# An expert's rows: gather products on TensorE, or an indirect DMA and transposes

## The chip, the cores and the metric

The kernel runs on one core of one Trainium2 chip. The metric is device microseconds from start to end of one execution; the median of three runs of the kernel before is 1578.53 us (1578.49 to 1578.84). The engines are TensorE (PE, with its weight loads as PEld), VectorE (DVE), ScalarE (ACT), GpSimd (POOL) and SyncE (SP). Each works through a queue of its own in order, and semaphores tie the queues together.

## The reference

A streaming encoder block on 512 tokens of width 1024. Attention, a recurrence and a first LayerNorm make `h`, 512 x 1024. Then comes the part that the change touches, a mixture of 32 experts of which each token uses four:

```python
logits = xt @ w_router + b_router
top_logit, top_e = lax.top_k(logits, 4); gate = softmax(top_logit)
# for each expert e, over the rows (tokens) that chose it:
hb = xb @ w_up[e] + b_up[e]                     # 1024 -> 2048
glu, lin = split(hb); glu = min(glu, 7); lin = clip(lin, -7, 7)
act = glu * sigmoid(1.702 * glu) * (lin + 1)
y = act @ w_down[e] + b_down[e]                 # 1024 -> 1024
out[token] += gate * y
h = layer_norm(ALPHA * h + out, ln2_g, ln2_b)
```

All of it is in float32; the weights of the 32 experts are 384 MB.

## The kernel before

**Slots.** Each expert has 128 slots, 32 for each of four blocks of 128 tokens. `posm` holds, for a token and an expert, the slot; `onehot` compares it with the slot numbers and makes `oh` for a group of four experts (`GRP`). `meta` multiplies `oh` with a small table `vals` and so gets each slot's token number (`idx`) and gate; an empty slot has a number above 511, which the indirect DMA skips.

**Rows.** `gather(k, n)` multiplies `h1` (128 of its 1024 columns) with `oh` for four experts at once, which gives the rows of these experts already transposed in PSUM. ScalarE writes the high part `xh[k]` and VectorE the remainder `xl[k]`, both in a 32-bit format that TensorE takes in one pass; three products (high x high, high x low, low x high) stand for one in float32 (`mm3`). For the first group the gather steps lie between the first expert's chunks; for a later group they lie in the last expert of the group before (`more`).

**Weights.** `Stream` brings the weights in chunks of 1 MB (128 x 2048) by SP into raw tiles: four of pool a, `RAW_B` = 2 and `RAW_C` = 1. An expert has eight up chunks and four down chunks; the order is up of expert e, then down of e - 1. A chunk is split by a ScalarE cast (line 88, high) and a VectorE subtract (line 90, low) into one of four pairs of tiles. `ahead(c)` puts the splits up to chunk c + 2 into the queues, and `raw` tiles set free take the next loads.

**The order in an expert.** `up_begin` starts four PSUM sums of 512 columns with a bias product each (line 401); `up_chunk` adds 12 products for each of eight chunks (lines 396 to 398). After chunk k come, in this order, `ahead(up[k])` and one step of `act_gen` of the expert before: transposes of its activation (`act_T`, lines 435, 438, 439) in two halves. Then `dn_half` adds the four down chunks of the expert before, twelve products each; behind chunk k come `ahead` and then a step of `act_gen` for the present expert: `act0` reads two sums on ScalarE (lines 419, 420), `act1` finishes on VectorE (lines 426 to 428), for half 0 and half 1. `u_buf`, one tile, is shared by both halves, so line 419 of half 1 waits for line 428 of half 0. `finish` scales the result on ScalarE (line 456) and POOL adds it into `acc` in DRAM by an indirect DMA (line 457). `final_tiles` prepares the last LayerNorm in raw tiles that are free once all weights are loaded.

**Before the experts.** A written order (`B_ORDER`) weaves the first LayerNorm, the router and the first four weight splits. `start_acc` scales a block of `h` on ScalarE into a tile `sl` and POOL stores it as the start of `acc`.

The instructions of all this are issued in program order on each engine, as written.

Of the kernel before, what the change touches and what calls it, by code (L numbers as in the profile page):

```python
# [157 lines left out]
class Moe:  # L158
    def __init__(self, tc, ctx, a, cst, ne=NE):
        self.tc, self.nc, self.a, self.c, self.ne = tc, tc.nc, a, cst, ne  # L160
        nc = tc.nc
        self.dram = ctx.enter_context(tc.tile_pool(name="moe_dram", bufs=1, space=DRAM))
        self.acc = self.dram.tile([T, D], F32, name="acc_dram")
        self.tab_f = self.dram.tile([128, 2], F32, name="tab_f")
        self.tab_i = self.dram.tile([128, 2], I32, name="tab_i")
        self.bias = ctx.enter_context(tc.tile_pool(name="moe_bias", bufs=1)).tile([128, 2048], BF, name="bias")

    def open_routing(self, ctx):
        tc = self.tc
        keep = ctx.enter_context(tc.tile_pool(name="moe_keep", bufs=1))  # L170
        self.small = ctx.enter_context(tc.tile_pool(name="moe_small", bufs=2))
        self.lg = keep.tile([128, NB, NE], F32, name="lg")
        self.mx = keep.tile([128, NB, 8], F32, name="mx")
        self.sel = keep.tile([128, NB, NE], BF, name="sel")
        self.posm = keep.tile([128, NB, NE], F32, name="posm")
        self.vals = keep.tile([128, NB, NE, 5], BF, name="vals")
        self.hT = {}
        self.n_i = keep.tile([128, 1], I32, name="n_i")
        hp = ctx.enter_context(tc.tile_pool(name="moe_h", bufs=1))
        self.hp = hp  # L180
        self.sl = [self.slot(b, [128, D], F32) for b in range(NB)]

    def slot(self, b, shape, dt):

        return self.hp.tile(shape, dt, name=f"sl{b}")
# [151 lines left out]
    def open(self, ctx, h1):  # L337
        tc, nc = self.tc, self.nc
        self.h1 = h1
# [6 lines left out]
        self.xh = [self.xp.tile([128, 128 * GRP], F32R, name=f"xh{k}", bufs=1) for k in range(8)]  # L346
        self.xl = [self.xp.tile([128, 128 * GRP], F32R, name=f"xl{k}", bufs=1) for k in range(8)]
# [3 lines left out]
        self.ohT = self.xh[0].rearrange("p (b t) -> p b t", b=NB)  # L351
# [7 lines left out]
    def meta(self, n, vals_of):  # L359

        nc = self.nc
        pm = self.ps_tr.tile([128, 4, 128], F32, name="ps_tr", tag="tr")
        ohb = self.oh.bitcast(BF).rearrange("p b e (j two) -> p b e j two", two=2)
        for i in range(n):
            for b in range(NB):
                nc.tensor.matmul(pm[SLB * b:SLB * b + SLB, 0, 8 * i:8 * i + 5], ohb[:, b, i, :, 1], vals_of(b, i),
                                 start=True, stop=True)
        yield
        m = self.xp.tile([128, GRP, 5], F32, name="meta")
        nc.vector.tensor_copy(m[:, 0:n], pm[:, 0, 0:8 * n].rearrange("p (i s) -> p i s", i=n)[:, :, 0:5])  # L370
        t = self.xp.tile([128, GRP], F32, name="meta_t")
        idx = self.xp.tile([128, GRP], I32, name="idx")
        nc.vector.scalar_tensor_tensor(t[:, 0:n], m[:, 0:n, 1], -BIG, m[:, 0:n, 0], op0=ALU.mult, op1=ALU.add)
        nc.vector.tensor_scalar(idx[:, 0:n], t[:, 0:n], self.c.base, None, op0=ALU.add)
        gate = self.xp.tile([128, GRP], F32, name="gate_s")
        nc.vector.tensor_reduce(gate[:, 0:n], m[:, 0:n, 2:5], axis=AX.X, op=ALU.add)
        self.where += [(idx[:, i:i + 1], gate[:, i:i + 1]) for i in range(n)]
# [31 lines left out]
    def up_chunk(self, ps, i, w, k):  # L409
        wh, wl = w  # L410
        xh, xl = (x[k][:, 128 * i:128 * i + 128] for x in (self.xh, self.xl))
# [97 lines left out]
    def slots_T(self, idx):  # L509

        nc = self.nc
        row = self.xp.tile([128, NB], F32, name="row")
        for b in range(NB):
# [46 lines left out]
    def experts(self, out):  # L560
# [7 lines left out]
        self.where = []  # L568
# [3 lines left out]
        def slots(e):  # L572
            self.onehot(self.posm[:, :, e:e + GRP], GRP)

        def rows(e):
            yield from self.meta(GRP, lambda b, i: self.vals[:, b, e + i, :])

        def act_gen(ps):
# [8 lines left out]
            t = [self.act_T(h) for h in range(2)]  # L587
            next(t[0])
            yield
            next(t[0])  # L590
            next(t[1])
            yield
            next(t[1])
            yield
# [6 lines left out]
        act = meta = iter(())  # L601
        for e in range(ne + 1):
            first, i = e == 0, e % GRP
            if e < ne:
                up = self.up_c[e]
                more = i == GRP - 1 and e + 1 < ne
                ps_up = self.up_begin(self.sel_of(e))
                gs = deque()
                for k in range(8):
                    if first and k < 7:  # L610
                        g = self.gather(k + 1, GRP)
                        next(g)
                    self.up_chunk(ps_up, i, st.get(up[k]), k)
                    if first and k < 7:
                        next(g)
                    ahead(up[k])
                    next(act, None)
                    if gs:
                        next(gs.popleft())
                    if more:  # L620
                        gs.append(self.gather(k, GRP))
                        next(gs[0])
                    if first and k == 0:
                        self.gate_parts()
                    if first and k in (1, 2, 3, 4):
                        self.start_acc(k - 1)
                    if first and k == 6:
                        meta = rows(0)
                    if i == GRP - 2 and k == 0 and e + 2 < ne:
                        slots(e + 2)  # L630
                        meta = rows(e + 2)
                    if k > 5:
                        next(meta, None)
            else:
                drain(act)
            if first:
                act = act_gen(ps_up)
                self.ah, self.al = (self.slot(b, [128, 8, 128], F32R) for b in (0, 1))
                self.y = self.slot(2, [128, D], F32)
                self.overflow_list(self.ps_tr, "tr")  # L640
                for _ in range(3):
                    next(act)
                continue
            ps = self.dn_begin()
            nxt = act_gen(ps_up) if e < ne else iter(())
            for k in range(4):
                w = st.get(self.dn_c[e - 1][k])
                self.dn_half(ps, w, k, 0)
                self.dn_half(ps, w, k, 1)
                ahead(self.dn_c[e - 1][k])  # L650
                if k < 3:
                    next(nxt, None)
                if k == 0 and gs:
                    next(gs.popleft())
            act = nxt
            if e < ne:
                self.finish(ps, *self.where[e - 1])
                self.added = e == ne - 1
        for _ in final:
            pass  # L660
        idx, gate = self.where[-1]
# [3 lines left out]
    def overflow(self, out):  # L665
# [3 lines left out]
        with tc.For_i(0, n, 1) as i:  # L669
# [23 lines left out]
            idx, gate = self.where[-1]  # L693
            for k in range(8):
                drain(self.gather(k, 1))
# [14 lines left out]
            for k in range(8):  # L710
                self.up_chunk(ps, 0, chunk(self.up_src(wu, k)), k)
# [891 lines left out]
RAW_B = 2  # L1603
RAW_C = 1
# [10 lines left out]
def build(tc, a, out):  # L1615
    nc = tc.nc
    with ExitStack() as ctx:
# [14 lines left out]
        with ExitStack() as c2:  # L1632
# [10 lines left out]
            def block(b):  # L1643
# [4 lines left out]
                def norm():  # L1648
                    ln.mean()
                    yield  # L1650
                    ln.squares(xb, moe.sl[b])
# [12 lines left out]
                def rest():  # L1664
# [6 lines left out]
                    ln.rest(xb, 1)  # L1671
                    yield
# [20 lines left out]
        with ExitStack() as c2:  # L1693
            st.grow([pool(c2, f"w_raw_c{i}", 1, "right", reuse_waits="tile") for i in range(RAW_C)])
            c2.enter_context(tc.manual_schedule())
            moe.open(c2, x)
# [17 lines left out]
```

## Time and profile before

| what | value |
| --- | --- |
| median of three runs | 1578.53 us |
| the profiled execution, its own time | 1581.11 us |
| its span, first to last instruction | 1579.3 us, mean granted clock 0.984 |
| TensorE busy | 1506.9 us (95%) |
| VectorE busy | 1321.6 us (84%) |
| ScalarE busy | 1077.5 us (68%) |
| HBM read | 430.48 MB, 287 GB/s over the span |
| plain POOL DMA issue (line 506) | 0.55 us of POOL |

The page gives busy time, share of the span and the number of instructions for each engine. TensorE's matmuls overlap each other, so its busy share says whether there are holes, not how near it is to its peak. Times in the trace count from the first instruction. The expert stage begins at 336.5 us (the first bias products) and the last down product of expert 30 starts at 1530.05 us.

### The profile page before, as it was taken

What the parts mean: (1) busy time and instruction counts of PE and PEld (TensorE: products, weight loads), DVE (VectorE), ACT (ScalarE), POOL (GpSimd) and SP (SyncE); (2) the same over time, 40 slices, a digit from 0 to 9 for tenths busy, and PEclk for the clock granted to TensorE, in tenths of its full rate; (3) what the DMA queues carried; (4) which work ended last, traced back from release to release, by engine and by line L of the source; (5) the groups of instructions that cost most, each with busy time, mean ns of one, the idle gap of its engine ahead of it and who ended that gap; (6) DMA issues with size and microseconds to landing.
All of it is one profiled execution on the core that took longest, in us unless ns stands there. A gap on an engine that the chain in (4) does not pass through costs nothing. (4 is left out here: it accounts for less than half of the span.)

```text
span 1579.3 us, 20360 instructions
## 1 busy us (share of the span) xinstructions
PE 1506.9 (95%) x7609; PEld 1243.3 (79%) x7641; DVE 1321.6 (84%) x1519; ACT 1077.5 (68%) x1148; POOL 163.2 (10%) x213
## 2 busy tenths in 40 slices
PE   7999999998999999999999999999999999999994
PEld 5888998876778878778878788878877887877873
DVE  8867877678888888889889979988988888888885
ACT  4678452456767777777677777777776777777762
POOL 5120413210000000000000000000000000000023
PEclk9999999999999999999999999999999999999997
DMA  5222117338898998899899979997999899889973
GB/s 194 90 71 67 28 41 271 138 138 298 336 338 309 368 372 308 335 364 356 299 353 352 359 280 366 369 368 282 374 371 332 311 371 373 311 336 363 353 257 113
DMA packets 95546, 446.67 MB, mean 283 GB/s; under 512 B 11407, under 2 KB 22072, under 8 KB 62674
## 3 DMA queue, kind: packets, MB, share of 16 engines
q1 hardware_dynamic: 86002, 425.51, 70.5%
q0 software_dynamic: 7488, 19.00, 4.9%
q8 instruction: 62, 1.02, 0.3%
q10 hardware_dynamic: 1952, 0.80, 0.2%
q14 instruction: 42, 0.34, 0.1%
HBM read 430.48 MB, written 22.55 MB: 287 GB/s over the span
## 5 line engine op out<-in xcount | busy, mean ns | idle before, releaser
L90 DVE TENSOR_TENSOR w_lo_t<-w_raw,w_hi_t 128x2048 fp32r<-128x2048 f32 (+1 forms) x392 | 877.9, 2269 | 155.5 <-ACT w_hi_t L88 155.5
L88 ACT CAST w_hi_t<-w_raw 128x2048 fp32r<-128x2048 f32 (+1 forms) x392 | 736.0, 1897 | 102.9 <-PE ps_up_t L398 88.7
L396 PE MATMUL ps_up_t<-w_hi_t,xh 128*128 128x512 f32 x1024 | 419.5, 410 | 0.0
L398 PE MATMUL ps_up_t<-w_hi_t,xl 128*128 128x512 f32 x1024 | 402.1, 393 | 0.0
L397 PE MATMUL ps_up_t<-w_lo_t,xh 128*128 128x512 f32 x1024 | 400.6, 391 | 0.0
L396 PEld LDWEIGHTS ps_up_t<-w_hi_t,xh 128*128 128x128 f32 x1024 | 193.2, 189 | 53.2 <-ACT sl L456 17.3
L398 PEld LDWEIGHTS ps_up_t<-w_hi_t,xl 128*128 128x128 f32 x1024 | 192.7, 188 | 44.4
L397 PEld LDWEIGHTS ps_up_t<-w_lo_t,xh 128*128 128x128 f32 x1024 | 193.3, 189 | 37.5
L396 PE MATMUL ps_dn_t<-w_hi_t,sl 128*128 128x512 f32 x512 | 202.7, 396 | 0.5 <-ACT sl L438 0.5
L398 PE MATMUL ps_dn_t<-w_hi_t,sl 128*128 128x512 f32 x512 | 201.4, 393 | 0.0
L397 PE MATMUL ps_dn_t<-w_lo_t,sl 128*128 128x512 f32 x512 | 200.8, 392 | 0.0
L457 POOL DMA_INDIRECT acc_dram<-sl,idx x31 | 48.5, 1563 | 1095.9 <-ACT sl L456 1041.6
L419 ACT ACTIVATE act_u<-ps_up_t 128x512 f32<-128x512 f32 x64 | 38.0, 594 | 130.0 <-DVE act_l L428 130.0
L398 PEld LDWEIGHTS ps_dn_t<-w_hi_t,sl 128*128 128x128 f32 x512 | 96.7, 189 | 22.0 <-DVE sl L439 0.3
L396 PEld LDWEIGHTS ps_dn_t<-w_hi_t,sl 128*128 128x128 f32 x512 | 96.9, 189 | 21.1 <-ACT sl L438 0.9
L397 PEld LDWEIGHTS ps_dn_t<-w_lo_t,sl 128*128 128x128 f32 x512 | 96.8, 189 | 21.0
L390 ACT CAST xh<-ps_tr 128x512 fp32r<-128x512 f32 x64 | 37.6, 588 | 66.1 <-PE ps_tr L386 66.1
L386 PEld LDWEIGHTS ps_tr<-oh,h 128*128 128x128 f32 x512 | 66.0, 191 | 6.0 <-DVE xl L391 1.3
L386 PE MATMUL ps_tr<-oh,h 128*128 128x128 f32 x512 | 68.4, 276 | 0.1
L438 ACT CAST sl<-ps_tr 128x512 fp32r<-128x512 f32 x64 | 37.5, 587 | 36.5 <-PE ps_tr L435 35.8
L919 PE MATMUL pj<-mw_hi,hT 128*128 128x256 f32 (+1 forms) x192 | 60.5, 315 | 1.6 <-ACT hT L1040 1.3
L920 PE MATMUL pj<-mw_lo,hT 128*128 128x256 f32 (+1 forms) x192 | 58.6, 306 | 1.1 <-DVE mw_lo L847 1.1
(360 smaller groups left out, 1786.4 us busy)
## 6 DMA issues: line engine op xcount, KB each, us to landing
w_raw<-in_w_up SPq DMA_DIRECT2D x256, 1024.0 KB
w_raw<-in_w_down SPq DMA_DIRECT2D x128, 1024.0 KB
mw_raw<-in_w_in SPq DMA_DIRECT2D x16, 512.0 KB
w_raw<-in_w_o SPq DMA_DIRECT2D x4, 1024.0 KB
mw_raw<-in_w_in SPq DMA_DIRECT2D x4, 672.0 KB
h_dram<-x POOLq DMA_DIRECT2D x4, 512.0 KB, 3.5
h<-h_dram POOLq DMA_DIRECT2D x4, 512.0 KB, 10.8
acc_dram<-sl POOLq DMA_DIRECT2D x4, 512.0 KB, 3.5
```

What stands on the lines that cost most here:

```text
L88: self.nc.scalar.copy(h[:, s], r[:, s])
L90: self.nc.vector.tensor_sub(l[:, s], r[:, s], h[:, s].bitcast(F32))
L386: nc.tensor.matmul(p[:, 0:n, SLB * b:SLB * b + SLB], self.h1[b][:, 128 * k:128 * k + 128], self.oh[:, b, 0:n, :], start=True, stop=True)
L390: nc.scalar.copy(self.xh[k][:, 0:128 * n], pf)
L396: mm(ps, xh, wh, start=start, stop=False)
L397: mm(ps, xh, wl, start=False, stop=False)
L398: mm(ps, xl, wh, start=False, stop=stop)
L419: nc.scalar.activation(self.u_buf, ps[h], AF.Sigmoid, scale=SW_ALPHA)
L438: nc.scalar.copy(ah[:, s, :], p)
L457: nc.gpsimd.indirect_dma_start(out=self.acc[:, :], out_offset=bass.IndirectOffsetOnAxis(ap=idx[:, :1], axis=0), in_=y, in_offset=None, bou ...
L919: mm(ps, xh, wh, start=start, stop=False, skip_group_check=True)
L920: mm(ps, xh, wl, start=False, stop=False, skip_group_check=True)
```

## The change

- Each block of `h` is stored to DRAM (`store_rows`, a DMA on POOL at the end of its LayerNorm). An expert's rows are fetched from there by `fetch`, an indirect DMA on POOL into one of two tiles `xg`, cleared at first; an empty slot leaves what stood there. The fetch of expert e + 1 is issued at the start of expert e; those of 0 and 1 before the first.
- `x_T` transposes the fetched rows in two blocks of four on TensorE; ScalarE and VectorE write `xh` and `xl` of that expert. It runs in the up chunks of the expert before (`turn`: first the two halves of `act_T`, then those of `x_T`, then `meta` of the next group).
- `gather` is gone. `meta` can give the index alone or the gate alone.
- After a chunk, up or down, the step (`turn`, or `halves` with `act0` and `act1`) now comes ahead of `ahead(...)`, that is, ahead of that chunk's weight split in the queues.
- The tiles `sl` are gone: `start_acc` scales `h1` in place, and the activation's tiles take the place of `h1`. `RAW_B` is 4 and `RAW_C` 2, so there are ten raw tiles in place of seven.

```diff
+    def store_rows(self, b, h):
+        self.nc.gpsimd.dma_start(self.rows[128 * b:128 * b + 128, :], h)
...
     def start_acc(self, b):
-        x = self.slot(b, [128, D], F32)
-        self.nc.scalar.mul(x, self.h1[b], ALPHA)
+        x = self.h1[b]
+        self.nc.scalar.mul(x, x, ALPHA)
         self.nc.gpsimd.dma_start(self.acc[128 * b:128 * b + 128, :], x)
...
+        self.xg = [self.xp.tile([128, D], F32, name=f"xg{i}", bufs=1) for i in range(2)]
+        for x in self.xg:
+            nc.gpsimd.memset(x, 0.0)
...
-    def gather(self, k, n):
-        p = self.ps_tr.tile([128, 4, 128], F32, name="ps_tr", tag="tr")
-        for b in range(NB):
-            nc.tensor.matmul(p[:, 0:n, SLB * b:SLB * b + SLB], self.h1[b][:, 128 * k:128 * k + 128],
-                             self.oh[:, b, 0:n, :], start=True, stop=True)
-        yield
-        pf = p.rearrange("p e t -> p (e t)")[:, 0:128 * n]
-        nc.scalar.copy(self.xh[k][:, 0:128 * n], pf)
-        nc.vector.tensor_sub(self.xl[k][:, 0:128 * n], pf, self.xh[k][:, 0:128 * n].bitcast(F32))
-        yield
+    def fetch(self, e, idx):
+        self.nc.gpsimd.indirect_dma_start(
+            out=self.xg[e % 2], out_offset=None, in_=self.rows[:, :],
+            in_offset=bass.IndirectOffsetOnAxis(ap=idx[:, :1], axis=0), bounds_check=T - 1, oob_is_err=False)
+
+    def x_T(self, e):
+        xh, xl = (self.xp.tile([128, 8, 128], F32R, name=nm) for nm in ("xh", "xl"))
+        self.x[e] = xh, xl
+        for q in range(2):
+            p = self.ps_tr.tile([128, 4, 128], F32, name="ps_tr", tag="tr")
+            for i in range(4):
+                k = 4 * q + i
+                nc.tensor.transpose(p[:, i, :], self.xg[e % 2][:, 128 * k:128 * k + 128], self.c.ident)
+            yield
+            s = slice(4 * q, 4 * q + 4)
+            nc.scalar.copy(xh[:, s, :], p)
+            nc.vector.tensor_sub(xl[:, s, :], p, xh[:, s, :].bitcast(F32))
+            yield
...
+        def turn():
+            if e:
+                t = [self.act_T(h) for h in range(2)]
+                next(t[0])
+                yield
+                next(t[0])
+                next(t[1])
+                yield
+                next(t[1])
+                yield
+            if e + 1 < ne:
+                t = self.x_T(e + 1)
+                next(t)
+                yield
+                next(t)
+                next(t)
+                yield
+                next(t)
+                yield
+            if first:
+                yield from meta(0, idx=False)
+            if e % GRP == 1 and e + GRP < ne:
+                slots(e // GRP + 1)
+                yield from meta(e // GRP + 1)
 
         slots(0)
+        drain(meta(0, gate=False))
+        for e in range(2):
+            self.fetch(e, self.idx[e])
         st.split_to(self.up_c[0][0] + FIRST_SPLIT)
-        g = self.gather(0, GRP)
-        next(g)
-        next(g)
+        drain(self.x_T(0))
         for e in range(ne + 1):
...
+                if e and e + 1 < ne:
+                    self.fetch(e + 1, self.idx[e + 1])
                 ps_up = self.up_begin(self.sel_of(e))
                 for k in range(8):
-                    self.up_chunk(ps_up, i, st.get(up[k]), k)
+                    self.up_chunk(ps_up, self.x[e], st.get(up[k]), k)
...
+                    next(steps, None)
                     ahead(up[k])
-                    next(act, None)
...
             for k in range(4):
                 w = st.get(self.dn_c[e - 1][k])
                 self.dn_half(ps, w, k, 0)
                 self.dn_half(ps, w, k, 1)
+                next(act, None)
                 ahead(self.dn_c[e - 1][k])
-                if k < 3:
-                    next(nxt, None)
...
-RAW_B = 2
-RAW_C = 1
+RAW_B = 4
+RAW_C = 2
...
                     ln.rest(xb, 1)
+                    moe.store_rows(b, xb)
                     yield
```

## Rows read from the trace of the kernel before

**Rows 1.** The page's busy time, share and instructions of each engine.

```profile
PE 1506.9 (95%) x7609; PEld 1243.3 (79%) x7641; DVE 1321.6 (84%) x1519; ACT 1077.5 (68%) x1148; POOL 163.2 (10%) x213
```

**Rows 2.** Table by stage, four experts: stretch, length, busy per engine, granted clock, DMA, GB/s.

```profile
1010.02:1045.52 35.50, 35.25 (x171) 28.25 (x172) 32.21 (x26) 26.82 (x21) 1.55 (x1) 1.00 0.96 363
1045.52:1089.38 43.86, 42.59 (x219) 35.28 (x220) 35.94 (x29) 30.30 (x29) 1.54 (x1) 1.00 0.83 298
1089.38:1124.93 35.55, 34.84 (x155) 28.14 (x156) 31.60 (x21) 27.03 (x22) 1.55 (x1) 1.00 0.93 359
1124.93:1160.07 35.14, 34.88 (x155) 28.15 (x156) 31.19 (x21) 26.58 (x21) 1.54 (x1) 1.00 0.96 368
```

**Rows 3.** Timeline of TensorE around a transpose block: start, length, instruction.

```profile
1013.53 0.40 PE L398 MATMUL ps_up_t<-w_hi_t,xl 128*128 128x512 f32 x1
...
1014.44 0.39 PE L397 MATMUL ps_up_t<-w_lo_t,xh 128*128 128x512 f32 x1
```

**Rows 4.** Timeline of TensorE: down products and next bias products; idle and releaser in brackets.

```profile
1034.30 0.39 PE L396 MATMUL ps_dn_t<-w_hi_t,sl 128*128 128x512 f32 x1
...
1042.77 0.39 PE L397 MATMUL ps_dn_t<-w_lo_t,sl 128*128 128x512 f32 x1
...
1045.06 0.40 PE L398 MATMUL ps_dn_t<-w_hi_t,sl 128*128 128x512 f32 x1
1045.52 0.59 PE L401 MATMUL ps_up_t<-bias,erow_b 128*128 128x512 bf16 x2
1046.29 0.38 PE L401 MATMUL ps_up_t<-bias,erow_b 128*128 128x512 bf16 x1 [0.17 <-DVE act_u L426]
```

**Rows 5.** Timeline of ScalarE around the end of the same expert.

```profile
1031.35 1.92 ACT L88 CAST w_hi_t<-w_raw 128x2048 fp32r<-128x2048 f32 x1 [0.83 <-PE ps_up_t L398]
...
1033.81 0.60 ACT L420 ACTIVATE act_l<-ps_up_t 128x512 f32<-128x512 f32 x1
1034.50 1.92 ACT L88 CAST w_hi_t<-w_raw 128x2048 fp32r<-128x2048 f32 x1
1040.44 0.60 ACT L419 ACTIVATE act_u<-ps_up_t 128x512 f32<-128x512 f32 x1 [4.02 <-DVE act_l L428]
...
1041.41 3.71 ACT L88 CAST w_hi_t<-w_raw 128x2048 fp32r<-128x2048 f32 x2
1045.01 1.27 ACT L456 ACTIVATE sl<-ps_dn_t,gate_s 128x512 f32<-128x512 f32 x2
```

**Rows 6.** Timeline of VectorE in the same stretch.

```profile
1036.45 2.29 DVE L90 TENSOR_TENSOR w_lo_t<-w_raw,w_hi_t 128x2048 fp32r<-128x2048 f32 x1 [0.20 <-ACT w_hi_t L88]
1038.66 0.68 DVE L426 SCALAR_TENSOR_TENSOR act_u<-ps_up_t,act_u 128x512 f32<-128x512 f32 x1
...
1043.35 2.29 DVE L90 TENSOR_TENSOR w_lo_t<-w_raw,w_hi_t 128x2048 fp32r<-128x2048 f32 x1 [2.94 <-ACT w_hi_t L88]
```

**Rows 7.** From issue to landing: the accumulates of line 457, the loads of line 506.

```profile
DMA to landing us min/median/max: 6.0/7.2/7.6
...
DMA to landing us min/median/max: 4.2/5.6/7.0
```

**Rows 8.** Timeline of VectorE and TensorE at the start of the expert stage.

```profile
334.38 0.69 DVE L356 TENSOR_TENSOR oh<-posm,slots 128x512 f32<-128x512 f32 x1
335.54 1.13 PE L386 MATMUL ps_tr<-oh,h 128*128 128x128 f32 x8
...
338.17 0.48 PE L396 MATMUL ps_up_t<-w_hi_t,xh 128*128 128x512 f32 x1
```

**Rows 9.** Table by stage, columns as in rows 2, around two falls of the clock.

```profile
35.30:39.50 4.20, 1.43 (x9) 1.10 (x9) 3.83 (x7) 1.78 (x8) 2.54 (x2) 1.00 0.00 0
39.60:42.90 3.30, 3.30 (x14) 3.25 (x13) 2.36 (x13) 1.74 (x5) 1.54 (x2) 0.50 0.01 2
367.40:370.60 3.20, 0.03 (x1) 0.00 (x0) 2.75 (x18) 0.00 (x0) 0.00 (x0) 1.00 0.99 355
370.70:377.40 6.70, 4.44 (x11) 2.91 (x11) 5.44 (x8) 4.67 (x4) 0.00 (x0) 0.50 0.35 132
```

**Rows 10.** Timeline of TensorE before the last transposes.

```profile
1533.47 0.64 PE L497 MATMUL ps_tr<-ident,w_raw 128*96 128x128 f32 x4 [3.02 <-POOL w_raw L485]
```

More of the change, by code (lines that the diff above doesn't have):

```diff
@@ L178, in open_routing @@
         self.n_i = keep.tile([128, 1], I32, name="n_i")
[L179 to L181 removed]
     def slot(self, b, shape, dt):
[L185 removed]
+        return self.h1_pool.tile(shape, dt, name=f"h1_{b}")
+    def store_rows(self, b, h):
+        self.nc.gpsimd.dma_start(self.rows[128 * b:128 * b + 128, :], h)
     def load_consts(self, pool):
@@ L371, in meta @@
[L371 to L377, printed above, removed]
@@ new lines, in meta @@
+        if idx:
+            t = self.xp.tile([128, GRP], F32, name="meta_t")
+            x = self.xp.tile([128, GRP], I32, name="idx")
+            nc.vector.scalar_tensor_tensor(t[:, 0:n], m[:, 0:n, 1], -BIG, m[:, 0:n, 0], op0=ALU.mult, op1=ALU.add)
+            nc.vector.tensor_scalar(x[:, 0:n], t[:, 0:n], self.c.base, None, op0=ALU.add)
+            self.idx += [x[:, i:i + 1] for i in range(n)]
+        if gate:
+            g = self.xp.tile([128, GRP], F32, name="gate_s")
+            nc.vector.tensor_reduce(g[:, 0:n], m[:, 0:n, 2:5], axis=AX.X, op=ALU.add)
+            self.gate += [g[:, i:i + 1] for i in range(n)]
@@ L567, in ahead, with meta, slots, halves @@
                 next(final, None)
-        self.where = []
+        self.idx, self.gate = [], []
         self.added = False
         ne = self.ne
[L572 to L578, printed above, removed]
+        def meta(g, **parts):
+            yield from self.meta(GRP, lambda b, i: self.vals[:, b, GRP * g + i, :], **parts)
+        def slots(g):
+            self.onehot(self.posm[:, :, GRP * g:GRP * g + GRP], GRP)
+        def halves(ps):
             self.act0(ps, 0)
@@ L596, in experts @@
         slots(0)
+        drain(meta(0, gate=False))
+        for e in range(2):
+            self.fetch(e, self.idx[e])
         st.split_to(self.up_c[0][0] + FIRST_SPLIT)
-        g = self.gather(0, GRP)
-        next(g)
-        next(g)
-        act = meta = iter(())
+        drain(self.x_T(0))
         for e in range(ne + 1):
-            first, i = e == 0, e % GRP
+            first = e == 0
+            steps = turn()
             if e < ne:
                 up = self.up_c[e]
-                more = i == GRP - 1 and e + 1 < ne
+                if e and e + 1 < ne:
+                    self.fetch(e + 1, self.idx[e + 1])
@@ L623, in experts @@
+                    if first and k in (1, 2, 3, 4):
+                        self.start_acc(k - 1)
+                    if first and k == 5:
+                        self.ah, self.al = (self.slot(b, [128, 8, 128], F32R) for b in (0, 1))
+                        self.y = self.slot(2, [128, D], F32)
+                    next(steps, None)
+                    ahead(up[k])
                     if first and k == 0:
                         self.gate_parts()
-                    if first and k in (1, 2, 3, 4):
-                        self.start_acc(k - 1)
@@ L627, in experts @@
[L627 to L635, printed above, removed]
+                del self.x[e]
+            drain(steps)
             if first:
-                act = act_gen(ps_up)
-                self.ah, self.al = (self.slot(b, [128, 8, 128], F32R) for b in (0, 1))
-                self.y = self.slot(2, [128, D], F32)
@@ L640, in experts @@
                 self.overflow_list(self.ps_tr, "tr")
-                for _ in range(3):
-                    next(act)
+                drain(halves(ps_up))
                 continue
             ps = self.dn_begin()
-            nxt = act_gen(ps_up) if e < ne else iter(())
+            act = halves(ps_up) if e < ne else iter(())
             for k in range(4):
@@ L649, in experts @@
                 self.dn_half(ps, w, k, 1)
+                next(act, None)
                 ahead(self.dn_c[e - 1][k])
-                if k < 3:
-                    next(nxt, None)
-                if k == 0 and gs:
-                    next(gs.popleft())
-            act = nxt
             if e < ne:
-                self.finish(ps, *self.where[e - 1])
+                self.finish(ps, self.idx[e - 1], self.gate[e - 1])
                 self.added = e == ne - 1
@@ L660, in experts @@
             pass
-        idx, gate = self.where[-1]
+        idx, gate = self.idx[-1], self.gate[-1]
         self.slots_T(idx)
@@ L692, in overflow @@
             drain(self.meta(1, lambda b, _: vals[:, b, :]))
-            idx, gate = self.where[-1]
-            for k in range(8):
-                drain(self.gather(k, 1))
+            idx, gate = self.idx[-1], self.gate[-1]
+            self.fetch(0, idx)
+            drain(self.x_T(0))
             et = self.xp.tile([128, NE], F32, name="ov_et")
```

48 lines of the change are left out of this document (15 added, 33 removed).

## The prediction

> **What bounds the kernel now.** I read the page first: TensorE is busy 95% of the span [rows 1]. Its matmuls overlap, so that share proves nothing yet. The table by stage comes next: from 409.93 to 1495.40 us the kernel repeats one pattern of four experts, 35.50, 43.86, 35.55 and 35.14 us long, 150.05 together [rows 2]. The long one makes the gather products for the next four. The timeline of TensorE says what fills a plain expert: from 1034.30 to 1045.06 there are 47 steps of 0.229 us without a hole [rows 4]. An expert has 96 up and 48 down products, 144 x 0.229 = 33.0 of 35.14 us; bias products, eight transposes and a short wait are the rest. So in this stage TensorE's own queue sets the time. VectorE's 31 to 32 us and ScalarE's 27 us lie beneath, and so do the weight loads: 368 GB/s in the plain expert, and yet no hole.
>
> How near the other engines are is the question; the view for it is the timeline of ScalarE and of VectorE around an expert's end [rows 5, 6]. The down products begin at 1034.30. ScalarE's cast at 1031.35 is that of down chunk 2; line 420 waits until 1033.81 for the last up sums that it reads; the cast at 1034.50 is chunk 3's; then line 419 waits 4.02 us for VectorE, which first subtracts chunk 3 (1036.45) and then runs lines 426 to 428 (from 1038.66). VectorE in turn waits 2.94 us for the next cast. TensorE sees none of it, because chunks 2 and 3 were sent ahead of these waits.
>
> **What is removed: the gather.** In the steady stage seven experts make 64 products each. Such an expert costs 43.86 - 35.14 = 8.72 us more than a plain one [rows 2], with the switches and a wait at the transposes in it. 7 x 8.72 = **-61.0 us**; the first expert's 56 products are in the start, below. ScalarE and VectorE gain nothing: eight 128x512 evacuations for four experts become two for each.
>
> **What is added: transposes.** `x_T` makes two blocks of four transposes an expert, in the shape of `act_T`. From the product at 1013.53 through such a block to the second product behind it, at 1014.44, is 0.91 us, where two plain steps take 0.46 [rows 3]. So 2 x 0.455 = 0.91 us in each of experts 1 to 30: **+27.3 us**. The index and gate products only move.
>
> **The fetch.** An indirect DMA per expert stands on POOL's queue right behind the accumulate of line 457. That one lands 7.2 us after its issue, at most 7.6 [rows 7]; it issues after the sums of 1045.01 [rows 5], about when up chunk 0 starts. The fetch, 1.55 us later on the queue [rows 2], is read after up chunk 3, some 12 us into the up products. Even if it lands 4.4 us behind the accumulate it fits, so I cost it at nothing; without that cover each us late is 30 us. More raw tiles only deepen a prefetch that is ahead already: nothing.
>
> **The moved evacuations: a gain.** `up_begin` waits for the last sums now: the third bias product starts at 1046.29, 0.77 us after the first, where two steps take about 0.44 [rows 4], so 0.33 is lost; after a gather expert it is another 0.41 (35.55 against 35.14). Sums that no longer stand behind one VectorE subtract (2.2 us) cover both. 30 x 0.33 + 7 x 0.41: **-13 us**.
>
> **The moved evacuations: a new wait.** In the new order ScalarE's queue at an expert's end is: sums of half 0, cast chunk 2, sums of half 1, cast chunk 3. VectorE's is: subtract 2, lines 426 to 428, subtract 3. Each piece waits for the one before it, and the first waits for TensorE's up sums. Forward from 1033.81 with the durations of [rows 5, 6]:
> - line 420 until its successor can start, 0.48 (half of 1040.44 to 1041.41): chunk 2's cast starts at 1034.29, not at 1031.35;
> - cast 1.92, subtract 2.21: line 426 at 1038.43;
> - lines 426 to 428 and the hand-over, 1.78 (1038.66 to 1040.44): line 419 at 1040.21;
> - lines 419 and 420, 0.97: chunk 3's cast at 1041.18, ready at 1043.1;
> - subtract 2.29: the low half of chunk 3 is ready at 1045.4.
>
> TensorE wants that half at 1042.77, with the second product of chunk 3 [rows 4]: it waits about 2.65 us, with one product in between. Chunk 2 is in time (wanted near 1040.0, ready at 1038.5). What is late next is up chunk 0: behind subtract 3 stand lines 426 to 428 and its own subtract, so it is ready at 1049.3; TensorE, ten steps and the bias products after 1045.4, wants it at 1049.05: 0.2 more. From there TensorE's chunk takes 2.75 us and VectorE's 2.2, and it catches up. The next expert starts the same chain from its own up sums, so the wait recurs. Per expert 2.85; bounds 2.2 (shorter hand-overs, chunk 0 in time) and 3.4 (both longer). Experts 1 to 30: **+85.5 us**; the last expert's is in the tail.
>
> **Start.** Now the one-hot ends at 335.07 and the first up product starts at 338.17 [rows 8]. After it come: sixteen tiny index products and three small vector operations (1.7 us, an estimate: one hand-over from the one-hot to TensorE, 335.54, is 0.47, and there are three), the fetch, a transpose block and its evacuation (1.5 us). For the fetch the nearest row is the plain POOL load of line 506, at least 4.2 us to landing [rows 7], plus 1.0 since an indirect issue holds POOL 1.55 us [rows 2] and a plain one 0.55: 5.2, bounds 4.2 and 7.6. So the first product comes near 343.5, +5.3. The first expert then lacks 56 products, 7/8 of 8.72 less a wait of 1.2: -6.5. It has one `x_T`, +0.9; the idle before it lets the clock fall, about +1.6 (half a stretch of rival 1); ScalarE's four scalings of 128x1024 have less TensorE time to hide in: +1.5. Sum **+3**, bounds -1 and +8 (fetch 7.6 us, or its tiles cleared late on POOL). The Trainium skill, "DMA: Bandwidth & Descriptors", section "Anatomy of one DMA — SWDGE (gpsimd) path", prices such a DMA at about 2.0 us plus bytes over 436 GB/s; for 512 KB that is an estimate of 3.2 us, and the sum by it would be 2 us lower. This trace shows 4.2 at best, and the row decides.
>
> **Tail.** TensorE now waits 3.02 us for POOL's bias work before the last activation's transposes [rows 10]. With three more raw tiles that POOL work starts about three chunks (8 us) earlier, so this wait goes (-3.0), the last sums come a subtract sooner (-2.2), and TensorE restarts with less idle before it (-1.6, as above); the last expert's stall takes 2.85 back. **-4**, bounds -6 and +1. `start_acc` in place, the rows' stores during the normalization (0.55 us of POOL each, where POOL waits for others) and their landing before the first fetch: nothing, at most 1 us.
>
> **Sum.** -61.0 + 27.3 - 13 + 85.5 + 3 - 4 = +37.8 us. The profiled execution took 1581.1 us (its span 1579.3 and 1.8 around it) and would take 1618.9; the median of the runs, 1578.53, is 2.6 below it, so I predict **1616 us**. Own range: 30 x (-0.65 to +0.55) for the stall, start and tail: 1590 to 1643.
>
> **Rivals.**
> 1. *The stall lowers the clock.* The wait is idle of 0.4 and 1.95 us with a product between. From 367.4 to 370.6 TensorE was busy 0.03 of 3.20 us, and the granted clock was 0.50, the 1.2 GHz level, for the next 6.7 us; from 35.3 to 39.5 it was busy 1.43 of 4.20 us, and the clock fell as well [rows 9]. The gather experts, idle 1.27 of 43.86 us in all, were granted 1.00 [rows 2]. Ours lies between. At half speed 6.7 us hold 15 steps instead of 29 and lose 3.1 us; falls in half the experts cost 15 x 3.1 = 47: **1663**. "TensorE: Matmul & The Clock Gate", Part 1, of the Trainium skill says that idle sends the array to half rate until activity is sustained again; the trace agrees at 367.4, and by that rule this rival comes true wherever such a stall counts as idle.
> 2. *No stall: faster.* If TensorE finds chunk 3 ready, the sum lacks 85.5: -48, **1531**. For it: the gather's 8.72 us are certain. Against it: the chain would have to be 2.65 us shorter, and every link is a row. It decides below a stall of (61 + 13 + 4 - 27.3 - 3)/30 = 1.6 us an expert; only then is the change faster.
> 3. *The fetch is late.* If accumulate and fetch take 7.6 us each, one after the other, the rows land 15.2 us after the accumulate's issue, wanted after some 12: 3.2 x 30 = 96, **1712**. Against it: both move only valid rows, and line 457 needs 7.6 at worst with weight loads beside it.
>
> **Chances.** Forecast 0.55; clock 0.27; no stall 0.13; late fetch 0.05. A difference under 0.2% (3.2 us) can't be told from none here. The no-stall case is faster 0.12 and, if part of the wait stays, same 0.01; a stall near 1.6 adds 0.01 to same; the rest, 0.86, is slower. The range leaves out no stall, the late fetch and the clock's worst: 1590 to 1672.
>
> **What would show it.** Plain experts take about 38.6 us, all four alike but for 0.4; TensorE has holes of 0.4 and 2 us around the first product of down chunk 3, released by lines 88 and 90; the wait of the bias products is gone; a transpose block costs 0.45; the granted clock stays at 1.00 from 420 to 1495 us. I am wrong if the down products run without a hole (period near 35.7), if the clock falls each period, or if the row transposes wait for the fetch.

## The result, and the profile after

The changed kernel takes 1778.38 us (four runs, 1774.73 to 1778.96) against 1578.51 us beside it: ratio 1.1264, 95% interval 1.1244 to 1.1283. That is slower, as forecast, but 162 us above the 1616 predicted and outside the range of 1590 to 1672. The profiled execution's span is 1777.1 us.

The page of the changed kernel, engines' busy time, answers to [rows 1]. TensorE falls from 95% to 88%: it has holes now.

```profile
PE 1557.7 (88%) x7368; PEld 1253.6 (71%) x7401; DVE 1334.0 (75%) x1520; ACT 1075.3 (61%) x1148; POOL 266.3 (15%) x251
```

The table by stage of the changed kernel, two whole experts (953.25 and 1084.15) and two short stretches in the first; columns as in [rows 2].

```profile
953.25:997.18 43.93, 39.32 (x163) 31.04 (x164) 33.15 (x23) 27.64 (x23) 4.45 (x2) 0.92 0.81 297
968.97:972.38 3.41, 3.41 (x10) 2.63 (x9) 1.87 (x2) 2.20 (x2) 0.00 (x0) 0.50 1.02 401
992.86:996.27 3.41, 3.41 (x9) 2.64 (x10) 3.38 (x4) 1.09 (x1) 0.00 (x0) 0.50 0.69 231
1084.15:1123.58 39.43, 36.94 (x179) 28.97 (x180) 31.39 (x27) 27.45 (x23) 4.45 (x2) 0.99 0.88 315
```

Instead of 35 us three times and 44 once, nearly every expert takes 39 to 48 us (mean of experts 2 to 30: 43.8). In the stage the granted clock falls to 0.50, the 1.2 GHz level, 37 times over experts 2 to 30: twice in 13 of these experts, once in 11, never in 5. Before, it never fell there.

The view of waits of the changed kernel, TensorE's own: what it waited for, us in total, times, longest.

```profile
PE ps_tr L402 <- DMA xg<-rows_dram,idx: 89.2, 28, 5.9
PE ps_dn_t L412 <- DVE w_lo_t L90: 54.8, 30, 1.8
PE ps_dn_t L411 <- ACT w_hi_t L88: 16.5, 30, 0.6
```

The second and third are the wait that was forecast, at down chunk 3. The first is the fetch (line 389; the row transposes are line 402), which was costed at nothing; 5.9 us of it are the very first fetch, in the start, and the other 83.3 lie in 27 of experts 2 to 30. The timeline of TensorE in the expert at 953.25 shows both places, first the row transposes, then down chunk 3 (down products are now lines 411 to 413, as the up products).

```profile
965.56 0.39 PE L413 MATMUL ps_up_t<-w_hi_t,xl 128*128 128x512 f32 x1
968.12 0.63 PE L402 MATMUL ps_tr<-ident,xg 128*128 128x128 f32 x4 [2.17 <-DMA xg<-rows_dram,idx]
...
989.48 0.39 PE L413 MATMUL ps_dn_t<-w_hi_t,h 128*128 128x512 f32 x1
990.40 0.49 PE L411 MATMUL ps_dn_t<-w_hi_t,h 128*128 128x512 f32 x1 [0.53 <-ACT w_hi_t L88]
992.73 0.70 PE L412 MATMUL ps_dn_t<-w_lo_t,h 128*128 128x512 f32 x1 [1.83 <-DVE w_lo_t L90]
```

From 989.48 to 992.73 are 3.25 us where two steps of 0.229 should stand: a stall of 2.80. In this expert each hole is followed by a stretch at half clock, 968.97 and 992.86 in the table above.

The timeline of ScalarE and of VectorE ahead of that stall answers to [rows 5, 6]. Half 1's sums come at 987.47, and the casts behind them (three in a row) only then; before, the cast of chunk 3 began 5.9 us ahead of line 419.

```profile
987.47 0.60 ACT L434 ACTIVATE act_u<-ps_up_t 128x512 f32<-128x512 f32 x1 [4.02 <-DVE act_l L443]
987.97 0.59 ACT L435 ACTIVATE act_l<-ps_up_t 128x512 f32<-128x512 f32 x1
988.44 5.50 ACT L88 CAST w_hi_t<-w_raw 128x2048 fp32r<-128x2048 f32 x3
```

```profile
985.70 0.68 DVE L441 SCALAR_TENSOR_TENSOR act_u<-ps_up_t,act_u 128x512 f32<-128x512 f32 x1
...
990.38 2.29 DVE L90 TENSOR_TENSOR w_lo_t<-w_raw,w_hi_t 128x2048 fp32r<-128x2048 f32 x1 [2.94 <-ACT w_hi_t L88]
```

POOL's timeline at the same expert's start, and VectorE's beside it: the accumulate (line 472) and the fetch behind it.

```profile
954.18 2.36 POOL L472 DMA_INDIRECT acc_dram<-h,idx  x1 [39.74 <-ACT h L471]
956.85 2.10 POOL L389 DMA_INDIRECT xg<-rows_dram,idx  x1 [0.30 <-issue]
```

```profile
950.58 4.49 DVE L90 TENSOR_TENSOR w_lo_t<-w_raw,w_hi_t 128x2048 fp32r<-128x2048 f32 x2
955.74 2.29 DVE L90 TENSOR_TENSOR w_lo_t<-w_raw,w_hi_t 128x2048 fp32r<-128x2048 f32 x1 [0.67 <-ACT w_hi_t L88]
```

And the issues of these two lines over the whole changed kernel, with the time from issue to landing (fetches, then accumulates).

```profile
L389 POOL DMA_INDIRECT xg<-rows_dram,idx x32: 1020/2018/2852, 342.2 to 1655.3; - x32
...
DMA to landing us min/median/max: 4.3/11.5/13.7
...
L472 POOL DMA_INDIRECT acc_dram<-h,idx x31: 1597/2365/3710, 423.1 to 1735.0; - x31
...
DMA to landing us min/median/max: 7.7/10.4/13.9
```

The accumulate, 7.2 us before [rows 7], now needs 10.4. The fetch, issued 2.67 us behind it, needs 11.5: it lands some 14 us behind the accumulate's issue, while TensorE wants the rows at 965.8, 11.6 us behind it. Paired expert by expert, the fetch lands 3.7 us after the accumulate ahead of it has landed (median of 29; 2.8 to 4.1).

### The profile page after: what moved, and what is told of

The parts are those of the page before. It is cut to its first block, busy times and chain, and to the rows that moved or that the text cites. A ratio compares the mean times of both kernels' runs of the same rounds, so it can differ in the third digit from the quotient of the medians.

```text
span 1777.1 us, 20021 instructions
## 1 busy us (share of the span) xinstructions
PE 1557.7 (88%) x7368; PEld 1253.6 (71%) x7401; DVE 1334.0 (75%) x1520; ACT 1075.3 (61%) x1148; POOL 266.3 (15%) x251
## 5 line engine op out<-in xcount | busy, mean ns | idle before, releaser
L472 POOL DMA_INDIRECT acc_dram<-h,idx x31 | 87.8, 2833 | 1193.6 <-ACT h L471 1193.6
L412 PE MATMUL ps_dn_t<-w_lo_t,h 128*128 128x512 f32 x512 | 214.8, 420 | 54.8 <-DVE w_lo_t L90 54.8
L412 PEld LDWEIGHTS ps_up_t<-w_lo_t,xh 128*128 128x128 f32 x1024 | 201.3, 197 | 43.8 <-DVE w_lo_t L90 4.9
L411 PE MATMUL ps_dn_t<-w_hi_t,h 128*128 128x512 f32 x512 | 212.8, 416 | 16.9 <-ACT w_hi_t L88 16.5
L413 PE MATMUL ps_dn_t<-w_hi_t,h 128*128 128x512 f32 x512 | 210.0, 410 | 1.3 <-DVE h L454 1.3
L412 PEld LDWEIGHTS ps_dn_t<-w_lo_t,h 128*128 128x128 f32 x512 | 103.0, 201 | 85.5 <-DVE w_lo_t L90 64.2
L411 PEld LDWEIGHTS ps_dn_t<-w_hi_t,h 128*128 128x128 f32 x512 | 102.0, 199 | 51.1 <-ACT w_hi_t L88 29.2
L402 PE MATMUL ps_tr<-ident,xg 128*128 128x128 f32 x256 | 45.2, 307 | 89.2 <-DMA xg<-rows_dram,idx 89.2
L406 DVE TENSOR_TENSOR xl<-ps_tr,xh 128x512 fp32r<-128x512 f32 x64 | 44.1, 690 | 105.2 <-ACT xh L405 104.9
L413 PEld LDWEIGHTS ps_dn_t<-w_hi_t,h 128*128 128x128 f32 x512 | 103.4, 202 | 23.0 <-DVE h L454 1.8
L402 PEld LDWEIGHTS ps_tr<-ident,xg 128*128 128x128 f32 x256 | 33.6, 157 | 105.1 <-issue 94.6
L453 ACT CAST h<-ps_tr 128x512 fp32r<-128x512 f32 x64 | 37.5, 587 | 82.6 <-PE ps_tr L450 82.6
L471 ACT ACTIVATE h<-ps_dn_t,gate_s 128x512 f32<-128x512 f32 x62 | 42.5, 688 | 55.7 <-PE ps_dn_t L413 55.5
```

Source lines behind the costliest of these rows:

```text
L402: nc.tensor.transpose(p[:, i, :], self.xg[e % 2][:, 128 * k:128 * k + 128], self.c.ident)
L406: nc.vector.tensor_sub(xl[:, s, :], p, xh[:, s, :].bitcast(F32))
L411: mm(ps, xh, wh, start=start, stop=False)
L412: mm(ps, xh, wl, start=False, stop=False)
L413: mm(ps, xl, wh, start=False, stop=stop)
L453: nc.scalar.copy(ah[:, s, :], p)
```

## The experiments

The first four separate two suspects, the order in the down loop and the place of the fetch. Each kernel is the changed one but for its diff; e4 starts from the kernel before. Of e1, e2, e4, e6 and e8 there is one run each, of the others four; the kernel before, run beside each group, took 1579.0 to 1579.4 us.

**e1: the down loop's order undone.**

```
                 self.dn_half(ps, w, k, 1)
-                next(act, None)
                 ahead(self.dn_c[e - 1][k])
+                next(act, None)
```

> The changed kernel, but behind a down chunk the weight split is queued first and the evacuation step second, as before the change; the fetch stays where it is. Theory A (two independent waits, at down chunk 3 by the queue order and at the row transposes by the late fetch, each with its own falls of the clock): the waits at down chunk 3, 81 us over experts 2 to 30, are gone, the bias products wait 0.33 us again (+10), and some 25 us of half-speed steps go with them: about 1680 us, with the transposes still waiting 2 to 5 us for the rows. Theory B (one budget: what is saved at chunk 3 is waited for at the transposes, because the period is set by transfers): 1760 us or more, transposes waiting 5 to 8 us.

Measured: 1599.34 us. Both theories missed, on the low side. The stall at chunk 3 is gone, and so, without being touched, is nearly all of the fetch's wait. In its place stands a wait of the bias products for VectorE's line 441, as [rows 4] but longer (1.41 us idle against 0.17):

```profile
PE ps_up_t L416 <- DVE act_u L441: 51.1, 31, 3.3
PE ps_tr L402 <- DMA xg<-rows_dram,idx: 7.2, 5, 5.9
```

```profile
944.29 0.59 PE L416 MATMUL ps_up_t<-bias,erow_b 128*128 128x512 bf16 x2
946.29 0.38 PE L416 MATMUL ps_up_t<-bias,erow_b 128*128 128x512 bf16 x1 [1.41 <-DVE act_u L441]
```

Of the fetch's 7.2 us, 5.9 are the first one, in the start.

**e2: the fetch earlier, the order as changed.** The fetch goes two experts ahead, behind up chunk 6, when its tile is free.

```
-                if e and e + 1 < ne:
-                    self.fetch(e + 1, self.idx[e + 1])
...
+                    if k == 6 and e + 2 < ne:
+                        self.fetch(e + 2, self.idx[e + 2])
```

> The changed kernel, but the rows of expert e + 2 are fetched in expert e (behind up chunk 6 in program order) in place of those of e + 1 at its start; the order of evacuation and split stays as changed. Theory A: the transposes no longer wait (-88 us), with 25 us of half-speed steps less: about 1665 us; the hole of 2.9 us at down chunk 3 stays in each expert. Theory B: the transfers set the period, and the wait turns up elsewhere, at the weight tiles: 1740 us or more. If the stall at chunk 3 alone makes the clock fall (the first rival of the prediction), the granted clock between 420 and 1690 us is under 0.97; if not, it is 1.00 there.

Measured: 1658.82 us. The row transposes wait no more, while the stall stays in every expert (54.9 and 16.6 us in its view of waits, 30 times each). The table by stage shows two of its experts, one with a fall of the clock and one without:

```profile
1017.80:1058.37 40.57, 37.87 (x179) 29.82 (x180) 33.76 (x28) 27.82 (x23) 4.46 (x2) 0.96 0.91 325
1058.38:1096.87 38.49, 36.05 (x164) 28.86 (x165) 31.22 (x22) 27.45 (x23) 4.45 (x2) 1.00 0.89 325
```

The prediction's plain expert was 38.6. The clock fell in 18 of experts 2 to 30, after the same stall as in the others; such an expert costs some 1.5 to 1.8 us more (40.0 to 40.3 where no `meta` is in it, expert 30 apart, against 38.4 to 38.7). So this kernel is the forecast plus rival 1, without the late fetch.

**e3: both edits.**

> Both edits together: split first behind a down chunk, and rows fetched an expert earlier. Theory A: no hole but the 0.33 us at the bias products; plain experts 36.0 us, granted clock 1.00; 1578.5 - 61 (gather) + 27 (transposes) + 8 (start): about 1552 us, faster than before. Theory B: not under 1600 us.

Measured: 1597.7 us, ratio 1.0118 (1.0101 to 1.0135): 1.6 us from e1, inside the 3.4 us over which its own runs lie. With the order undone the place of the fetch is worth nothing that can be measured; with the changed order it is worth 119.6 us. The 1552 expected failed, because the wait of e1's bias products is here too (51.0 us).

**e4: the changed order alone, in the kernel before** (gather and all): the same two lines swapped in its down loop.

> The kernel before, gather products and all, with one edit: behind a down chunk the evacuation step is queued ahead of the weight split. Theory A: the hole of 2.9 us at down chunk 3 appears in the experts 1 to 30 without any fetch, the bias products stop waiting (-13), and so 1578.5 + 30 x 2.9 - 13 = 1652 us, up to 1690 if the clock falls. Rival (the hole needs the transposes of the rows or the deeper prefetch as well): within 15 us of 1578.5.

Measured: 1669.73 us, 90 slower than before. The stall appears without any fetch or transposes (idle of 56.6 us for line 90 and 10.7 for line 88), and a plain expert goes from 35.14 to 37.82 us:

```profile
1020.17:1057.99 37.82, 35.48 (x155) 27.98 (x156) 31.24 (x21) 26.91 (x21) 3.64 (x1) 1.00 0.90 341
```

The row has one more thing: POOL's one instruction, the accumulate, holds it 3.64 us instead of 1.55 [rows 2], and lands after a median of 11.3 us instead of 7.2, with no fetch in the kernel. So the order also slows the accumulate. The clock fell 12 times over experts 2 to 30, which is part of why the time lies above the 1652.

The next five ask what is left in e3, what makes the fetch late, and what the deeper prefetch gives. "Up order" means that in the up loop, too, the changed kernel put the evacuations ahead of the split.

**e5: e3 with the last sums' step ahead of its split.**

```
+                if k == 2:
+                    next(act, None)
                 ahead(self.dn_c[e - 1][k])
-                next(act, None)
+                if k < 2:
+                    next(act, None)
```

> e3's kernel with one edit: in the down product loop the last of the three evacuation steps (the up sums' second half) goes ahead of the third chunk's weight split, the other two stay behind theirs. Theory A: the 1.75 us that the bias products still wait in an e3 expert come from this one step lying behind a 4 us split on VectorE; ahead of it, it fits into VectorE's idle time and the bias wait goes to 0.4 or less, without a new hole at down chunk 3 (which came from the first two sums' steps queued ahead of the casts). Then a plain expert takes 35.7 us (37.05 less 1.35), 29 of them some 45 us less than e3's, and the time is near 1552. Theory B: any sums step ahead of a split makes the next down chunk late: a hole of 1 us or more at the last down chunk, the clock falls again, and the time is 1590 or more.

Measured: 1565.31 us, ratio 0.9909 (0.9893 to 0.9926). Theory A holds for the bias wait, which is gone, but a plain expert takes 36.16 us and not 35.7: VectorE is late as before, and the lateness moved to the second product of up chunk 0 (here in the expert behind a `meta`; 0.9 us between the two products in the others):

```profile
711.03 0.58 PE L411 MATMUL ps_up_t<-w_hi_t,xh 128*128 128x512 f32 x1
712.93 0.50 PE L412 MATMUL ps_up_t<-w_lo_t,xh 128*128 128x512 f32 x1 [1.33 <-DVE w_lo_t L90]
```

**e6: e3 with the up order undone.**

```
-                    next(steps, None)
                     ahead(up[k])
+                    next(steps, None)
```

> e3's kernel with one edit: in the up product loop the weight split goes ahead of the transposes' evacuations again, as in the kernel before. Theory A: it was this order that made VectorE later by some 1.2 us at the expert's end; with it undone the bias wait falls from 1.75 to near the 0.57 of before, the period from 37.05 to 35.9, the time to about 1565. Theory B: it is the two more VectorE evacuations that each expert now has, wherever they are queued: the bias wait stays within 0.3 us of 1.75 and the time within 8 us of e3's 1597.7.

Measured: 1559.52 us. The bias wait falls from 51.0 to 13.2 us, and a plain expert from 37.09 to 36.06:

```profile
PE ps_up_t L416 <- DVE act_u L441: 13.2, 31, 3.3
```

So the up order held VectorE back; 35.9 was expected. 38 us of e3's time hung on it.

**e7: e5's and e6's edits together.**

> Both edits, e5's and e6's, on e3's kernel. Theory A: no wait is left in a plain expert but the 0.4 us at its first up products; within 5 us of e5's time (near 1552), and at 35.6 us a plain expert. Theory B: with the transposes' evacuations behind a split, the x transposes or the first down products wait for them, 0.5 us or more per expert, and it is 10 us or more slower than e5.

Measured: 1540.23 us, ratio 0.9760 (0.9744 to 0.9776): faster than the kernel before. It came out 25 us below e5, and not within 5, since e5 had kept a wait. Four of its experts in the table by stage, against 150.05 us for four before [rows 2]:

```profile
950.72:986.71 35.99, 35.92 (x180) 29.01 (x180) 33.83 (x28) 27.74 (x23) 4.45 (x2) 1.00 0.96 367
986.71:1022.27 35.56, 35.50 (x163) 28.91 (x164) 32.72 (x23) 27.41 (x23) 4.46 (x2) 1.00 0.95 369
1022.27:1057.84 35.57, 35.50 (x163) 28.92 (x164) 32.80 (x23) 27.46 (x23) 4.46 (x2) 1.00 0.97 370
1057.84:1093.41 35.57, 35.50 (x164) 28.92 (x164) 32.76 (x23) 27.45 (x23) 4.46 (x2) 1.00 0.95 368
```

They take 142.69 us, and TensorE is busy in all but 0.07 us of each. None of the waits for lines 88, 90 or 441, or for the fetch, is left in this stage. The accumulates are slow here too (a median of 2.75 us to issue and 11.0 to land), and the early fetch hides it; no run has these orders with the fetch behind the accumulate.

**e8: no accumulate, the order as changed.**

```
-        nc.gpsimd.indirect_dma_start(
-            out=self.acc[:, :], out_offset=bass.IndirectOffsetOnAxis(ap=idx[:, :1], axis=0),
-            in_=y, in_offset=None, bounds_check=T - 1, oob_is_err=False, compute_op=ALU.add)
```

> The changed kernel without the accumulate of 31 experts (the indirect DMA that adds an expert's rows to the sums in DRAM is left out, so the sums hold the last expert and the starting rows alone); everything else, the order of sums and split included, as in the changed kernel. Theory A: the fetch is late because it is queued on POOL and in the DMA queues right behind the accumulate: without it the fetch's issue is back to 1.0 to 1.6 us, it lands within 6 us, and the row transposes' wait of 87.6 us over 29 experts falls under 15; the stall at down chunk 3 (2.8 us per expert) stays; time near 1665, as when the fetch was issued early (1658.8). Theory B: the fetch is late because of the weight stream alone: it still lands after 9 us or more, the waits stay above 50 us, and the time above 1710.

Measured: 1657.69 us, as e2. Its view of waits, and the fetches' own:

```profile
PE ps_tr L402 <- DMA xg<-rows_dram,idx: 5.9, 1, 5.9
```

```profile
  PE ps_tr L402: 727.9, 21
...
DMA to landing us min/median/max: 4.3/7.5/10.2
```

The first line of the second fence says what 21 of POOL's 32 fetches waited for: the transposes that last read their tile, an expert earlier. With no accumulate ahead of it on POOL's queue the fetch goes out when its tile is free and is never late. The issue stays at a median of 2.14 us, where 1.0 to 1.6 was expected, and it lands in 7.5, not 6. So without the accumulate ahead of it the stage's whole wait is gone (5.9 us are the first fetch), but the fetch is still slower than expected; that is the last section's.

**e10: e7 with the raw tiles of before** (`RAW_B` 2, `RAW_C` 1).

> The kernel with both orders (e7) with the number of raw weight tiles put back from 4 and 2 to 2 and 1: the one part of the change that no run has yet undone, and that the prediction put at nothing. Theory A: the weight stream is 0.8 us or more ahead of its split in every chunk, so the deeper queue of loads gives nothing: within 4 us of e7's 1540.2, experts at 35.56 us. Theory B: with three raw tiles fewer loads are in flight while the fetch and the accumulate take their share of the DMA engines, and a split waits for its chunk: 10 us or more slower than e7, with waits for the raw tiles in the chain of VectorE or ScalarE.

Measured: 1538.24 us, ratio 0.9736 (0.9720 to 0.9752); the intervals of e7 and e10 overlap. The deeper queue of loads gives nothing in this kernel's stage, as predicted. Only in the tail does it show: the last transposes wait 5.6 us for POOL's bias work here, 3.3 in e7.

## Why the prediction was wrong

The two suspects side by side (us):

| | fetch behind the accumulate | fetch early |
| --- | --- | --- |
| sums ahead of the split (changed) | 1778.4 | e2: 1658.8 |
| split ahead of the sums (down loop) | e1: 1599.3 | e3: 1597.7 |

**The stall** was right: forecast 2.85 us an expert, at down chunk 3, released by lines 88 and 90; measured 2.80. e1 and e4 show that the order alone makes and unmakes it. This is why the sign was right.

**The fetch** is the step that failed: "Even if it lands 4.4 us behind the accumulate it fits, so I cost it at nothing". The step let the rows land 4.4 us behind an accumulate of 7.2 us, 7.6 at most, so 11.6 to 12.0 us from its issue; TensorE allows 11.6 in the expert shown. The 4.4 were enough: the fetch lands 3.7 us behind the accumulate. The 7.2 were not: the accumulate takes 10.4, both together some 14, and TensorE waits 89 us (83 in the stage). The step took the accumulate's 7.2 us from a kernel in which VectorE, at that moment, had no subtract running, and moved that subtract in the same sum without asking POOL. There the subtract of chunk 3 ends at 1045.64, before the scaled sums, at 1046.28, let the accumulate go [rows 5, 6]; in the new order VectorE is still subtracting then. e4 (3.6 us to issue, 11.3 to land, no fetch) against before, and e1 (1.6 and 6.6, fetch behind it) against the changed kernel, show that the order slows the accumulate; the time from its landing to the fetch's is no longer in the changed kernel (3.7 us) than in e1 (5.0). e2 and e8 show that a fetch that doesn't stand behind the accumulate is not late, and e1 that one behind an accumulate of 6.6 us hardly is.

**The clock** (rival 1, 0.27) came true as well: 18 falls in e2 and 37 in the changed kernel over experts 2 to 30; in e2 each expert has one stall, in the changed kernel 27 of the 29 have the wait for the fetch as well. Priced at 3.1 us, a fall costs 1.5 to 1.8 in e2.

**The chances** shared the error: forecast, rival 1 and rival 3 stood as alternatives, but all three follow from one cause, the order in the down loop, and came together: e1 undoes it, and the stall, all but 1.3 us of the stage's wait for the fetch, and all falls of the clock but one are gone. 1616 + 47 + 96 = 1759 is near the result, and the range ended at 1672. From bias product to bias product of experts 2 to 31 the stage grew from 1085.5 to 1270.5 us, by 185.0. The gather's, the transposes' and the bias wait's terms for these 29 experts give -47; the stall 81; the wait for the fetch 88, counted from product to product as the stall is (83.3 of it idle); the clock between 50 (an estimate, from the half-speed steps) and 72 (half of the 143 us at that level). That is 172 to 194.

**No stall** (rival 2, 1531) is what e7 does: 1540. Gather out, transposes in, and the bias wait gone add up as forecast: a plain expert was to take 35.14 + 0.91 - 0.33 = 35.72 and takes 35.56. The 9 us above 1531 come from the start and the tail: forecast at -1 together, they cost 10 here (expert 2 begins 6.2 us later than before, and the last bias products stand 87.5 us before the end, not 83.9). Against them the stage between came out 5 us shorter than forecast (1033.7 us, before 1085.5). The up loop's order, which the prediction did not price, makes no wait of the bias products in the changed kernel (3.3 us, once); with the down loop's order undone it is worth 38 us (e3 to e6).

**Start**: +3 forecast, +6.9 measured at expert 1 (its bias products at 373.90, before 367.05), inside the bounds. POOL clears the two tiles exactly while VectorE routes the last block:

```profile
333.50 1.87 POOL L350 MEMSET xg<- 128x1024 f32 x2 [5.19 <-DVE lg L240]
...
333.56 0.92 DVE L245 TENSOR_SCALAR gt<-lg,mx 128x32 f32<-128x32 f32 x1
...
338.00 0.69 DVE L359 TENSOR_TENSOR oh<-posm,slots 128x512 f32<-128x512 f32 x1
```

Line 245 takes 0.24 us in the blocks before this one, line 248 then 0.79 instead of 0.23: 1.2 us of the 3.6 by which the one-hot is later than in [rows 8]. Each of the two ends 0.04 us after the memset beside it does (334.44 and 335.37), so they were held until it was done. The other 2.4 us were lost before that block's routing; no run was made on either. The fetch itself took 4.3 us to land, as its row's lower bound had it.

**Tail**: -4 forecast, +0.3 measured (last bias products to end, 84.2 against 83.9). POOL's bias work did come earlier, nearly as forecast: its first cast starts 24.2 us after the last bias products, in the kernel before 31.4. But the last transposes come earlier too: the product ahead of their wait starts 26.2 us after the last bias products, in the kernel before 34.7, since with more raw tiles free `final_tiles` puts its transposes into TensorE's queue sooner (e10, with the tiles of before, has that product at 34.3, e7 at 26.0). So the wait did not go: 4.2 us, before 3.02 [rows 10]. The first line below is the kernel before, the others the changed one.

```profile
1526.81 1.04 POOL L480 CAST w_raw<-w_raw 96x1024 fp32r<-96x1024 f32 x1 [6.66 <-DMA w_raw<-in_b_down]
...
1709.86 1.63 POOL L489 DMA_DIRECT2D w_raw<-in_b_down  x3 [12.33 <-DVE w_lo_t L90]
1717.12 1.04 POOL L495 CAST w_raw<-w_raw 96x1024 fp32r<-96x1024 f32 x1 [5.63 <-DMA w_raw<-in_b_down]
...
1719.11 0.39 PE L413 MATMUL ps_dn_t<-w_hi_t,h 128*128 128x512 f32 x1
```

## What to carry to other kernels

When an edit moves an engine's work in time, take no duration of another engine's overlapping instruction over from the old trace unchanged: look at what ran beside it there, and what will. Rivals that follow from one cause are not alternatives; price them together and let the range reach to their sum. And work that waits (a sum to be read) belongs behind work that doesn't wait (a split whose data is there), in each loop by itself: with the new order undone in both loops, but for the one step that fits into idle time, and with the fetch early, this change makes the kernel 2.4% faster, not 12.6% slower.

## What the runs showed of the hardware

**An indirect DMA's issue waits for VectorE's subtract.** In the changed kernel a subtract of line 90 is running when 29 of 31 accumulates start, and each issue ends 1.46 to 1.53 us after that subtract does (after the second, where two follow each other). In the rows of the profile after: two subtracts from 950.58 end at 955.07, the issue at 956.54. In e1 and e3 no accumulate meets a running subtract, and all take 1.57 to 1.67 us. e5 differs from e3 by one step's place, so that each accumulate meets one:

```profile
L472 POOL DMA_INDIRECT acc_dram<-h,idx x31: 1573/1597/1674, 419.0 to 1551.0; - x31
...
DMA to landing us min/median/max: 6.2/6.7/10.2
```

```profile
L472 POOL DMA_INDIRECT acc_dram<-h,idx x31: 2731/2758/2825, 421.9 to 1521.0; - x31
...
DMA to landing us min/median/max: 7.6/11.0/12.7
```

The first fence is e3, the second e5. The landing comes 4.3 us later, more than the 1.2 us of the issue. The subtract isn't slowed: two in a row beside an issue take 4.49 us, no more than twice the 2.29 of [rows 6]. The Trainium skill, "SBUF — State Buffer", section "SBUF: two separate sides", states that VectorE and GpSimd share a pair of ports as an exclusive lock, which a VectorE operation with two SBUF inputs takes against a GpSimd operation that reads SBUF, and that GpSimd cannot write DMA descriptors while VectorE holds the ports. These rows agree in that direction. In the other they show no hold: in e3 a subtract starts 0.66 us into every issue and takes its 2.28 us all the same; what did hold VectorE was a memset of POOL's (Start, above). No run here shows which part of the later landing is descriptors and which is the weight loads beside them. Each fetch's issue but the first two meets a running subtract, in all kernels looked at (e1, e2, e8 and the changed one), so what a fetch costs without one, under the weight loads, stays open.

**Which hole lowers the clock.** Holes of 0.54 to 0.62 and 1.83 us with one product between them were followed by a stretch at the 1.2 GHz level in 18 of 29 experts of e2, and in the other 11, at 0.54 and 1.83, were not. Holes at the bias products, 1.36 to 1.41 us in three experts of four and 2.26 to 2.37 in the fourth, lowered it nowhere from 456 to 1505 us in e1, and twice in e3, both times after one of the longer kind.
